# First stage of a streaming-encoder block: another reciprocal root, adaLN sums of two blocks on TensorE, and the last gate sums moved

## The chip, the cores and the metric

The kernel runs on one core of a Trainium2 chip. The metric is the device time of one execution in microseconds, as the median of several runs. The profile is that of one execution, whose own time stands beside its span.

## The reference, cut to what matters

The block takes x (1024 rows of 1024) and a conditioning row c (1024). Its first part is an adaLN-modulated RMS normalisation:

```
ada = c @ w_ada + b_ada                     # 1024 x 3072
shift, scale, gate = split(ada, 3)
h = x * rsqrt(mean(x*x, -1) + 1e-6) * norm_w * (1 + scale) + shift
proj = h @ w_in                             # cq, ckv, k_rope, gates, q_b, k_b, v_b, ...
... two attentions, gated, merged, projected back ...
x = x + gate * (merged @ w_out)
```

All arithmetic is fp32. A product of two fp32 matrices is made of three passes over a high and a low part of each operand (hi x hi, hi x lo, lo x hi). The change is about `rsqrt`, about `c @ w_ada` for the first two blocks of 128 channels (of shift and scale), and about where in the program a part of `c @ w_ada` for `gate` is summed.

## The kernel before, in words

x lies in eight tiles of 128 rows. In the first stage (`phase0`) ScalarE squares a tile and sums along its rows (`square`, L269); for each pair of tiles VectorE makes the reciprocal root and scales both tiles (`scale`, L272, L276). `rsqrt` (L84 to L97) starts from a bit trick and takes three Newton steps, eleven VectorE operations that each need the one before. TensorE then transposes a tile in eight pieces of 128x128 (`turn`, L285) into PSUM, and ScalarE copies them to xT (`evac`, L301).

A block kt is 128 channels of xT. For it the kernel needs one shift and one gain per channel, which are sums over the 1024 entries of c. There are two ways for one such sum: `ada_rows` (L303) gives it to TensorE as eight matmuls of 64 equal columns, each run in two passes (x16 in the trace), and `ada_cols` (L311) to VectorE, as a product with c (a copy of it on all partitions, cb) that sums along its row. Before, only the shift of block 0 goes by TensorE. `gain` (L315) finishes the two numbers. `high`, `modulate` and `low` (L322 to L336) make the high part of h on ScalarE, h itself, and the low part on VectorE. `products` (L344) are the three passes of the first projection (cq, 424 columns) for a block and some tiles. TensorE makes the products of blocks kt0 and kt1 for six of the eight tiles and then for the two last ones, and goes on with block kt2.

The order is written out by hand: the calls in `phase0`, one after the other, give each engine its order. All loads are issued by one queue (SP) in that order; the order of loads is thus the order of the calls `load_x`, `load` and `load_cq`. TensorE begins with 32 transposes of the identity (`warm`).

Later, with the latents made, a loop over sp (L1384) makes keys; in each of its four turns two of the eight blocks of `gate` are summed on VectorE (`gate_sum`, L873, L878). In between, `fill_to` lets TensorE do other projections (passes over b), whose results VectorE makes ready with bv_u (L830). The last sums are ahead of one of these bv_u in VectorE's order. Then `attention` opens: rope and transposes of queries and keys (q_u, k_u, ks_u, kt), and after it a fixed table of steps; `gate_row` (L882) stands in it at step (2, 0) and transposes the eight sums on TensorE.

Of the kernel before, what the change touches and what calls it, by code (L numbers as in the profile page):

```python
# [10 lines left out]
F32 = mybir.dt.float32  # L11
# [3 lines left out]
AF = mybir.ActivationFunctionType  # L15
ALU = mybir.AluOpType
# [9 lines left out]
EPS = 1e-6  # L26
# [48 lines left out]
class Net:  # L75
# [78 lines left out]
    def consts(self):  # L154
        nc, t, U = self.nc, self.t, self.U
        cp = self.cp
        self.x0 = U.get([P, D], F32, "x0")
        nc.sync.dma_start(self.x0, t["x"][0:P, :])
        self.ident = cp.tile([P, P], F32, name="ident")
        nc.sync.dma_start(self.ident, t["ident"])  # L160
        self.vec = cp.tile([P, t["vec"].shape[1]], F32, name="vec")
        nc.sync.dma_start(self.vec, t["vec"])
        self.misc_raw = self.Hs.get([P, 512], F32, "misc")
        self.pos = cp.tile([P, ST], I32, name="pos")
        self.ones = cp.tile([P, 1], F32, name="ones")
# [12 lines left out]
        self.bf_row = v[:, 41:49]
        self.b_gate = v[:, 49:57]
# [59 lines left out]
    def phase0(self):  # L239
# [11 lines left out]
        def load_x(*sts):  # L251
            for st in sts:
                xs[st] = U.get([P, D], F32, f"x{st}")
                nc.sync.dma_start(xs[st], t["x"][st * P:(st + 1) * P, :])

        def load(kt):
            wada[kt] = [U.get([P, D], F32, f"wada{kt}{e}") for e in range(2)]
            for e in range(2):
                nc.sync.dma_start(wada[kt][e], t["w_ada"][kt][:, e])

        def load_cq(gi, half=None):
            if not half:
                cqw.append(U.get([P, 2, 424], F32, f"raw_cq{gi}"))
            k = slice(0, 2) if half is None else slice(half, half + 1)
            nc.sync.dma_start(cqw[gi][:, k], t["w_cq"][:, 2 * gi + k.start:2 * gi + k.stop])

        def square(st):
            junk = Hs.get([P, 512], F32, f"junk{st}")
            nc.scalar.activation(junk.bitcast(BF16), xs[st], AF.Square, accum_out=ssq[:, st:st + 1])  # L269
            Hs.put(junk)  # L270

        def scale(pair):  # L272
            a, b = pair
            r = self.rsqrt(ssq[:, a:b + 1], 2, D, f"x{a}")
# [27 lines left out]

        def ada_rows(kt, bank):  # L303

            pa = self.bank(bank, f"pada{kt}")[:, 0:64]
            w = wada[kt][0].rearrange("p (r c) -> p r c", r=8)
            for rc in range(8):
                self.mm(pa, w[:, rc], col(rc).broadcast_to([P, 64]), rc == 0, rc == 7)
            return pa[:, 0:1]

        def ada_cols(kt, e):  # L311
            w, a = wada[kt][e], acc[:, kt, e:e + 1]
            nc.vector.scalar_tensor_tensor(out=w, in0=w, scalar=1.0, in1=self.cb, op0=ALU.mult, op1=ALU.mult, accum_out=a)

        def gain(kt, a0=None):  # L315
            a0, a1 = acc[:, kt, 0:1] if a0 is None else a0, acc[:, kt, 1:2]
            nc.vector.tensor_scalar(out=gs[:, kt, 0:1], in0=a0, scalar1=self.b_shift[:, kt:kt + 1], scalar2=None, op0=ALU.add)
            nc.vector.scalar_tensor_tensor(out=gs[:, kt, 1:2], in0=a1, scalar=self.b1[:, kt:kt + 1],
                                           in1=self.nw[:, kt:kt + 1], op0=ALU.add, op1=ALU.mult)
            U.put(*wada.pop(kt))  # L320
# [29 lines left out]
        self.gcol = self.sp.tile([P, 8], F32, name="gcol")  # L350
        load_x(1, 2, 3, 4, 5)
        load(0)
        self.cb = U.get([P, D], F32, "cb")
        nc.sync.dma_start(self.cb, t["c_row"].broadcast_to([P, D]))
        load_cq(0, 0)
        load_x(6, 7)
        load(1)
        load_cq(0, 1)
        most, last = range(6), (6, 7)
        self.warm_bank = self.bank("f", "warm")  # L360
        for st in range(5):
# [12 lines left out]
        a0 = ada_rows(0, "o")
        evac(2)
        square(6)
        ada_cols(0, 1)
        gain(0, a0)
        load(2)
        evac(3)  # L380
        wh, wl = U.get([P, 2, 424], F32R, "hi_cq0"), U.get([P, 2, 424], F32R, "lo_cq0")
        nc.scalar.copy(wh[:, 0], cqw[0][:, 0])
        high(0, range(4))
        scale((4, 5))
        modulate(0, range(4), "d")
# [3 lines left out]
        turn(4, "tt")
        evac(4)  # L390
        square(7)
        turn(5, "of")
        evac(5)
        high(0, (4, 5))
        scale((6, 7))
        accs = [self.bank("s", f"cq_s{i}") for i in range(2)]
        for st in range(4):
            banks[st] = accs[st // 2][:, st % 2 * 512:st % 2 * 512 + 512]
        products(0, range(4), (0, ))
        load(3)  # L400
        load_cq(2)
        nc.sync.dma_start(self.misc_raw[:, 0:t["misc"].shape[1]], t["misc"])
        nc.sync.dma_start(self.pos, t["pos"])
        products(0, range(4), (2, 1))
        turn(6, "tt")
        evac(6)
        turn(7, "tt")
        modulate(0, (4, 5), "d")
        low(0, (4, 5))
        banks[4], banks[5] = self.bank("o", "cq_o"), self.bank("f", "cq_f")  # L410
        products(0, (4, 5))
        ada_cols(1, 0)
        ada_cols(1, 1)
        gain(1)
        high(1, most)
        modulate(1, most, "a")
        nc.scalar.copy(wh[:, 1], cqw[0][:, 1])
        evac(7)
        nc.vector.tensor_tensor(out=wl[:, 1], in0=cqw[0][:, 1], in1=wh[:, 1].bitcast(F32), op=ALU.subtract)
        U.put(cqw[0])  # L420
        load(4)
        low(1, most)
        products(1, most)
        wh, wl = U.get([P, 2, 424], F32R, "hi_cq1"), U.get([P, 2, 424], F32R, "lo_cq1")
        ada_cols(2, 0)
        ada_cols(2, 1)
# [800 lines left out]
    def attention(self):  # L1227
# [92 lines left out]
    def build(self):  # L1320
# [91 lines left out]
def layout(i):  # L1412
# [68 lines left out]
```

## Time and profile before

| | us |
|---|---|
| median of 3 runs (lowest, highest) | 979.08 (977.92, 980.4) |
| the profiled execution's own time | 978.43 |
| its span | 976.3 |
| TensorE busy in the span | 950.1 (97%) |
| VectorE busy | 642.2 (66%) |
| ScalarE busy | 477.0 (49%) |
| GpSimd busy | 203.4 (21%) |

The span is from the first to the last instruction of the profiled execution. The idle time of an engine that waits for nothing late costs nothing; what counts is where TensorE, which is busy nearly all the time, stands still or has a lower clock. PEclk is the granted clock as a share of full speed: 1.00 is 2.4 GHz, 0.50 is 1.2 GHz. DMA shares are of 16 engines.

### The profile page before, as it was taken

How to read it: one execution, taken by the hardware profiler on the slowest of the kernel's cores; microseconds unless marked ns; L12 is line 12 of the kernel's file. 1: busy time of each engine (PE TensorE's matmuls, PEld its weight loads, DVE VectorE, ACT ScalarE, POOL GpSimd, SP SyncE). 2: the span in 40 equal slices, each digit the busy share in tenths (PEclk: the TensorE clock that was granted, in tenths of full speed). 3: DMA queues.
4: the chain of work that ended last, by engine and by line, in shares of the span. 5: the costliest groups of instructions: out<-in, count | busy, mean ns of one | idle time of the engine just before them, and what ended most of it. 6: DMA issues, size and time to landing. Idle time of an engine off the chain costs nothing.

```text
span 976.3 us, 15256 instructions
## 1 busy us (share of the span) xinstructions
PE 950.1 (97%) x5534; PEld 829.2 (85%) x5534; DVE 642.2 (66%) x1408; ACT 477.0 (49%) x955; POOL 203.4 (21%) x259
## 2 busy tenths in 40 slices
PE   5899999999999999999999999999999999999998
PEld 5799999999897887888888888888888878887887
DVE  5877877777645756667667677667676757496222
ACT  6775824443244555656555566565565644143000
POOL 0013024300002221222233323332333210045000
PEclk9999999999999999999999999999999999999999
DMA  9831032854954224225323232232411554643321
GB/s 349 312 98 44 23 109 83 295 193 160 312 163 130 87 65 109 87 65 141 98 76 100 66 88 67 93 105 88 131 56 44 184 183 151 225 152 130 105 90 65
DMA packets 80987, 124.98 MB, mean 128 GB/s; under 512 B 5928, under 2 KB 47536, under 8 KB 80912
## 3 DMA queue, kind: packets, MB, share of 16 engines
q1 hardware_dynamic: 80912, 124.01, 38.6%
q8 instruction: 43, 0.70, 0.3%
q14 instruction: 32, 0.26, 0.1%
HBM read 88.33 MB, written 35.66 MB: 127 GB/s over the span
## 4 chain that ended last, share of the span: by engine, by line
PE 62%; DVE 3%; DMA 2%; issue 1%; ACT 0%; SPq 0%; ACTq 0%; DVEq 0%
PE f L127 31%; PE out L127 9%; PE s L127 8%; PE o L127 7%; PE pt L136 6%; DMA raw_f_u<-in_w_br 1%; DVE hT_lo L986 1%; DVE mg_h L979 1%; PE kt L136 1%; PE qt L136 1%; DMA mg_h<-mg_d 1%; DVE lo_f_u L116 1%; ACT p_u L1160 0%; ACT q_u L1096 0%; ACT hi_f_u L115 0%
## 5 line engine op out<-in xcount | busy, mean ns | idle before, releaser
L1180 ACT CAST pp_u<-pt 128x512 fp32r<-128x512 f32 x192 | 91.9, 479 | 179.3 <-PE pt L136 164.1
L1181 DVE TENSOR_TENSOR pp_u<-pt,pp_u 128x512 fp32r<-128x512 f32 x192 | 106.5, 555 | 76.4 <-ACT pp_u L1180 74.5
L127 PE MATMUL f<-hT_lo,hi_f_u 128*128 128x512 f32 x384 | 153.5, 400 | 0.0
L127 PE MATMUL f<-hT_hi,lo_f_u 128*128 128x512 f32 x384 | 153.3, 399 | 0.0
L127 PE MATMUL f<-hT_hi,hi_f_u 128*128 128x512 f32 x384 | 153.3, 399 | 0.0
L127 PE MATMUL s<-k_u,q_u 96*128 96x512 f32 (+6 forms) x480 | 116.5, 362 | 2.0 <-ACT p_u L1160 1.2
L127 PE MATMUL b<-hi_b_u,hT_hi 128*128 128x256 f32 x384 | 110.4, 288 | 2.3 <-DVE bv_u L830 2.3
L127 PE MATMUL b<-lo_b_u,hT_hi 128*128 128x256 f32 x384 | 109.2, 284 | 0.0
L127 PE MATMUL b<-hi_b_u,hT_lo 128*128 128x256 f32 x384 | 109.2, 284 | 0.0
L1154 DVE TENSOR_REDUCE nm<-s 128x1 f32<-128x128 f32 (+7 forms) x128 | 97.0, 758 | 4.4
L1164 POOL TENSOR_SCALAR p_u<-p_u,rs 128x640 f32<-128x640 f32 (+1 forms) x64 | 64.4, 1006 | 166.7 <-DVE rs L1163 83.5
L127 PE MATMUL o<-pp_u,v_u 128*128 128x512 f32 (+7 forms) x384 | 94.2, 340 | 0.0
L1164 POOL TENSOR_SCALAR p_h<-p_h,rs 128x128 f32<-128x128 f32 (+1 forms) x64 | 36.7, 573 | 252.1 <-DVE rs L1163 205.9
L127 PEld LDWEIGHTS s<-k_u,q_u 96*128 96x128 f32 (+2 forms) x480 | 76.6, 190 | 7.6 <-ACT p_u L1160 1.5
L127 PEld LDWEIGHTS f<-hT_hi,lo_f_u 128*128 128x128 f32 x384 | 72.4, 189 | 11.9
L127 PEld LDWEIGHTS f<-hT_lo,hi_f_u 128*128 128x128 f32 x384 | 72.4, 189 | 11.5
L127 PEld LDWEIGHTS f<-hT_hi,hi_f_u 128*128 128x128 f32 x384 | 72.5, 189 | 11.0
L127 PEld LDWEIGHTS o<-pp_u,v_u 128*128 128x128 f32 (+1 forms) x384 | 61.7, 161 | 19.9 <-DVE pp_u L1181 0.4
L127 PEld LDWEIGHTS b<-hi_b_u,hT_hi 128*128 128x128 f32 x384 | 74.3, 193 | 2.8 <-DVE bv_u L830 2.5
L127 PEld LDWEIGHTS b<-lo_b_u,hT_hi 128*128 128x128 f32 x384 | 74.3, 194 | 0.3
L127 PEld LDWEIGHTS b<-hi_b_u,hT_lo 128*128 128x128 f32 x384 | 74.2, 193 | 0.0
L136 PEld LDWEIGHTS pt<-ident,p_u 128*128 128x128 f32 x416 | 52.7, 140 | 16.4
(306 smaller groups left out, 1997.6 us busy)
## 6 DMA issues: line engine op xcount, KB each, us to landing
raw_f_u<-in_w_t SPq DMA_DIRECT2D x24, 512.0 KB
wada_u<-in_w_ada SPq DMA_DIRECT2D x16, 512.0 KB
mg_d<-th_h SPq DMA_DIRECT2D x32, 256.0 KB
mg_h<-mg_d SPq DMA_DIRECT2D x32, 256.0 KB
raw_b_u<-in_w_b SPq DMA_DIRECT2D x12, 512.0 KB
x_u<-in_x SPq DMA_DIRECT2D x8, 512.0 KB
raw_wg_u<-in_w_gate SPq DMA_DIRECT2D x8, 512.0 KB
va_d<-vhl_u SPq DMA_DIRECT2D x8, 512.0 KB
```

The lines of the kernel that those rows point to most:

```text
L116: engine.tensor_tensor(out=lo[:, ks], in0=raw[:, ks], in1=hi[:, ks].bitcast(F32), op=ALU.subtract)
L127: self.nc.tensor.matmul(out, lhsT=l, rhs=r, start=start, stop=stop)
L136: self.nc.tensor.transpose(out=out, in_=in_, identity=self.ident)
L979: nc.vector.scalar_tensor_tensor(out=m, in0=m, scalar=1.0, in1=acc, op0=ALU.add, op1=ALU.mult)
L986: nc.vector.tensor_tensor(out=self.hT_lo[x], in0=mA[c1][:, x[2]], in1=self.hT_hi[x].bitcast(F32), op=ALU.subtract)
L1154: nc.vector.tensor_reduce(out=nm, in_=sv, axis=AX.X, op=ALU.max, negate=True)
L1164: nc.gpsimd.tensor_scalar(out=p[:, 0:w], in0=p[:, 0:w], scalar1=rs, scalar2=0.0, op0=ALU.mult, op1=ALU.add)
L1180: nc.scalar.copy(ph[:, c0:], pt[:, c0:])
L1181: nc.vector.tensor_tensor(out=pl[:, c0:], in0=pt[:, c0:], in1=ph[:, c0:].bitcast(F32), op=ALU.subtract)
```

## The change

The root of a pair of tiles is made by ScalarE's Sqrt and VectorE's reciprocal, then one Newton step; a first Sqrt of a constant is issued before the first square, so that the activation table is there. Both sums of block 0 and both of block 1 go by TensorE (four times eight narrow matmuls, where one stood). The first two pairs are scaled straight after their squares. Loads: x6 and x7 go ahead of c's row and the first projection weights, block 1's weights are loaded ahead of c's row, and block 4's ahead of two small ones. The sums of four gate blocks (4 to 7) move from the loop to the opening of `attention`, and `gate_row` from step (2, 0) to (3, 0).

```diff
@@ scale
-            r = self.rsqrt(ssq[:, a:b + 1], 2, D, f"x{a}")
+            v, y, q = (...)
+            nc.vector.tensor_scalar(out=v, in0=ssq[:, a:b + 1], scalar1=1.0 / D, scalar2=EPS, op0=ALU.mult, op1=ALU.add)
+            nc.scalar.activation(y, ssq[:, a:b + 1], AF.Sqrt, scale=1.0 / D, bias=self.eps)
+            nc.vector.reciprocal(y, y)
+            nc.vector.scalar_tensor_tensor(out=q, in0=y, scalar=-0.5, in1=y, op0=ALU.mult, op1=ALU.mult)
+            nc.vector.tensor_tensor(out=q, in0=q, in1=v, op=ALU.mult)
+            nc.vector.scalar_tensor_tensor(out=y, in0=q, scalar=1.5, in1=y, op0=ALU.add, op1=ALU.mult)
+            r = y
@@ ada_rows
-            pa = self.bank(bank, f"pada{kt}")[:, 0:64]
-            w = wada[kt][0].rearrange("p (r c) -> p r c", r=8)
-            for rc in range(8):
-                self.mm(pa, w[:, rc], col(rc).broadcast_to([P, 64]), rc == 0, rc == 7)
-            return pa[:, 0:1]
+            b = self.bank(bank, f"pada{kt}")
+            for e in range(2):
+                w = wada[kt][e].rearrange("p (r c) -> p r c", r=8)
+                for rc in range(8):
+                    self.mm(b[:, 64 * e:64 * e + 64], w[:, rc], col(rc).broadcast_to([P, 64]), rc == 0, rc == 7)
+            return b[:, 0:1], b[:, 64:65]
@@ the order of phase0
         load(0)
+        load_x(6, 7)
+        load_cq(0, 0)
+        load(1)
+        load_cq(0, 1)
         self.cb = U.get([P, D], F32, "cb")
         nc.sync.dma_start(self.cb, t["c_row"].broadcast_to([P, D]))
-        load_cq(0, 0)
-        load_x(6, 7)
-        load(1)
-        load_cq(0, 1)
+        load_cq(1)
...
-        for st in range(5):
+        nc.scalar.activation(root, self.eps, AF.Sqrt)
+        for st in range(4):
             square(st)
+            if st % 2:
+                scale((st - 1, st))
         warm(32, self.ident)
-        scale((0, 1))
...
-        a0 = ada_rows(0, "o")
         evac(2)
+        rows = ada_rows(0, "o")
+        evac(3)
+        gain(0, rows)
         square(6)
-        ada_cols(0, 1)
-        gain(0, a0)
...
-        products(0, range(4), (0, ))
+        products(0, range(4), (0, 2))
+        rows = ada_rows(1, "t")
+        modulate(0, (4, 5), "d")
+        low(0, (4, 5))
+        gain(1, rows)
+        nc.scalar.copy(wh[:, 1], cqw[0][:, 1])
+        products(0, range(4), (1, ))
...
-        ada_cols(1, 0)
-        ada_cols(1, 1)
-        gain(1)
-        high(1, most)
-        modulate(1, most, "a")
@@ attention's opening
         self.load_v(0)
+        self.gate_sum(range(4, 8))
+        self.U.put(self.cb)
@@ the loop over sp, and the table of steps
-                    self.gate_sum((2 * sp, 2 * sp + 1))
+                    if sp < 2:
+                        self.gate_sum((2 * sp, 2 * sp + 1))
...
-        self.extra += [((2, 0), self.gate_row, ())]
+        self.extra += [((3, 0), self.gate_row, ())]
```

VectorE, first pair of x in the first stage, before (v, y and a are the root's tiles, x_u a tile of x):

```order
L88 TENSOR_SCALAR v_x_182<-xssq 128x2
L89 TENSOR_SCALAR y_x_183<-v_x_182 128x2
L93 SCALAR_TENSOR_TENSOR a_x_184<-y_x_183 128x2
L95 TENSOR_TENSOR a_x_184<-a_x_184,v_x_182 128x2
L96 SCALAR_TENSOR_TENSOR y_x_183<-a_x_184,y_x_183 128x2
L93 SCALAR_TENSOR_TENSOR a_x_184<-y_x_183 128x2
L95 TENSOR_TENSOR a_x_184<-a_x_184,v_x_182 128x2
L96 SCALAR_TENSOR_TENSOR y_x_183<-a_x_184,y_x_183 128x2
L93 SCALAR_TENSOR_TENSOR a_x_184<-y_x_183 128x2
L95 TENSOR_TENSOR a_x_184<-a_x_184,v_x_182 128x2
L96 SCALAR_TENSOR_TENSOR y_x_183<-a_x_184,y_x_183 128x2
L276 TENSOR_SCALAR x_u_1_87<-x_u_1_87,y_x_183 128x1024
```

VectorE at the same place now:

```order
L278 TENSOR_SCALAR v_x_150<-xssq 128x2
L280 RECIPROCAL y_x_151<-y_x_151 128x2
L281 SCALAR_TENSOR_TENSOR a_x_152<-y_x_151 128x2
L282 TENSOR_TENSOR a_x_152<-a_x_152,v_x_150 128x2
L283 SCALAR_TENSOR_TENSOR y_x_151<-a_x_152,y_x_151 128x2
L286 TENSOR_SCALAR x_u_1_87<-x_u_1_87,y_x_151 128x1024
L286 TENSOR_SCALAR x_u_2_114<-x_u_2_114,y_x_151 128x1024
L278 TENSOR_SCALAR v_x_165<-xssq 128x2
```

Five operations lie ahead of the first scaling where eleven did, and the Sqrt that feeds the reciprocal is on ScalarE. TensorE, from the first narrow matmuls (pada) to the second group of products, before (xt are transposes, cq_s products of the first four tiles):

```order
L127 MATMUL pada_260<-vec,wada_u_7_122 128x64 x8
L136 MATMUL xt_0_305<-ident,x_u_5_118 128x128 x4
L136 MATMUL xt_1_306<-ident,x_u_5_118 128x128 x4
L136 MATMUL xt_0_319<-ident,x_u_6_120 128x128 x4
L136 MATMUL xt_1_320<-ident,x_u_6_120 128x128 x4
L127 MATMUL cq_s_348<-hi_cq_u_18_282,hT_hi 128x424 x2
L127 MATMUL cq_s_349<-hi_cq_u_18_282,hT_hi 128x424 x2
L127 MATMUL cq_s_348<-hi_cq_u_18_282,hT_lo 128x424 x2
L127 MATMUL cq_s_349<-hi_cq_u_18_282,hT_lo 128x424 x2
```

TensorE at the same place now:

```order
L127 MATMUL pada_267<-vec,wada_u_7_124 128x64 x8
L127 MATMUL pada_267<-vec,wada_u_8_125 128x64 x8
L136 MATMUL xt_0_294<-ident,x_u_5_120 128x128 x4
L136 MATMUL xt_1_295<-ident,x_u_5_120 128x128 x4
L136 MATMUL xt_0_304<-ident,x_u_6_122 128x128 x4
L136 MATMUL xt_1_305<-ident,x_u_6_122 128x128 x4
L127 MATMUL cq_s_343<-hi_cq_u_16_291,hT_hi 128x424 x2
L127 MATMUL cq_s_344<-hi_cq_u_16_291,hT_hi 128x424 x2
L127 MATMUL cq_s_343<-hi_cq_u_16_291,hT_lo 128x424 x2
L127 MATMUL cq_s_344<-hi_cq_u_16_291,hT_lo 128x424 x2
L127 MATMUL pada_353<-vec,wada_u_12_134 128x64 x8
L127 MATMUL pada_353<-vec,wada_u_13_135 128x64 x8
```

Both sums of block 0 stand ahead of the transposes of x4 and x5, and both of block 1 stand between the products of block 0. VectorE around the last two gate sums (raw_wg_u), before (bv_u makes a projection of b ready, kraw_h are keys, q_u queries):

```order
L788 TENSOR_TENSOR kraw_h_64_2984<-kraw_h_64_2984,y_g2k_3050 128x512
L788 TENSOR_TENSOR kraw_h_65_3042<-kraw_h_65_3042,y_g2k_3050 128x512
L878 SCALAR_TENSOR_TENSOR raw_wg_u_132_2878,gcol<-raw_wg_u_132_2878,cb_u_112_2410 128x1024
L878 SCALAR_TENSOR_TENSOR raw_wg_u_133_2880,gcol<-raw_wg_u_133_2880,cb_u_112_2410 128x1024
L830 TENSOR_TENSOR bv_1_u_141_3101<-b_1_3010,bv_1_u_141_3101 128x8x64
L116 TENSOR_TENSOR lo_b_1_u_143_3106<-raw_b_1_u_135_2925,hi_b_1_u_142_3105 128x512 x2
L830 TENSOR_TENSOR bv_2_u_145_3170<-b_2_3111,bv_2_u_145_3170 128x8x64
L830 TENSOR_TENSOR bv_3_u_146_3223<-b_3_3174,bv_3_u_146_3223 128x8x64
L1047 SCALAR_TENSOR_TENSOR q_0_u_150_3263<-qt_3270,vqa,q_0_u_149_3262 64x512
```

VectorE at the same place and at the new place now:

```order
L800 TENSOR_TENSOR kraw_h_64_2988<-kraw_h_64_2988,y_g2k_3054 128x512
L800 TENSOR_TENSOR kraw_h_65_3046<-kraw_h_65_3046,y_g2k_3054 128x512
L842 TENSOR_TENSOR bv_1_u_141_3103<-b_1_3014,bv_1_u_141_3103 128x8x64
L116 TENSOR_TENSOR lo_b_1_u_143_3108<-raw_b_1_u_135_2929,hi_b_1_u_142_3107 128x512 x2
L842 TENSOR_TENSOR bv_2_u_145_3172<-b_2_3113,bv_2_u_145_3172 128x8x64
L842 TENSOR_TENSOR bv_3_u_146_3225<-b_3_3176,bv_3_u_146_3225 128x8x64
L890 SCALAR_TENSOR_TENSOR raw_wg_u_126_2715,gcol<-raw_wg_u_126_2715,cb_u_112_2416 128x1024
L890 SCALAR_TENSOR_TENSOR raw_wg_u_127_2717,gcol<-raw_wg_u_127_2717,cb_u_112_2416 128x1024
L890 SCALAR_TENSOR_TENSOR raw_wg_u_132_2882,gcol<-raw_wg_u_132_2882,cb_u_112_2416 128x1024
L890 SCALAR_TENSOR_TENSOR raw_wg_u_133_2884,gcol<-raw_wg_u_133_2884,cb_u_112_2416 128x1024
L1059 SCALAR_TENSOR_TENSOR q_0_u_150_3269<-qt_3276,vqa,q_0_u_149_3268 64x512
L1059 SCALAR_TENSOR_TENSOR q_1_u_152_3273<-qt_3276,vqa,q_1_u_151_3272 64x512
```

No gate sum is ahead of the first bv_u now; four stand behind the third one, ahead of the first q_u.

## Rows read from the trace of the kernel before

**Rows 1.** The page's busy time, share of the span and instructions of each engine

```profile
PE 950.1 (97%) x5534; PEld 829.2 (85%) x5534; DVE 642.2 (66%) x1408; ACT 477.0 (49%) x955; POOL 203.4 (21%) x259
```

**Rows 2.** Windows: stretch, length, busy time, PEclk, DMA share, GB/s

```profile
10.20:20.40 10.20, 6.50 (x56) 5.89 (x54) 7.58 (x30) 8.30 (x17) 0.00 (x0) 1.00 1.03 403
20.50:27.20 6.70, 4.59 (x20) 4.55 (x21) 4.86 (x17) 4.61 (x10) 0.00 (x0) 0.50 1.04 409
259.40:262.70 3.30, 3.02 (x14) 3.02 (x15) 2.03 (x4) 0.00 (x0) 0.00 (x0) 0.50 0.98 336
270.00:278.00 8.00, 7.99 (x68) 7.80 (x67) 3.69 (x5) 3.32 (x5) 0.00 (x0) 1.00 0.92 257
```

**Rows 3.** Timeline, TensorE, 10 to 42: start, length, what, [idle before]

```profile
12.05 1.97 PE L136 MATMUL xt<-ident,x_u 128*128 128x128 f32 x16 [1.02 <-DVE x_u L276]
15.55 1.97 PE L136 MATMUL xt<-ident,x_u 128*128 128x128 f32 x16 [1.53 <-DVE x_u L276]
17.35 1.90 PE L127 MATMUL pada<-vec,wada_u 128*128 128x64 f32 x16
22.61 3.65 PE L136 MATMUL xt<-ident,x_u 128*128 128x128 f32 x16 [3.36 <-DVE x_u L276]
...
27.37 0.93 PE L127 MATMUL cq_s<-hi_cq_u,hT_lo 128*128 128x424 f32 x4
28.14 0.93 PE L127 MATMUL cq_s<-lo_cq_u,hT_hi 128*128 128x424 f32 x4
...
35.77 1.04 PE L127 MATMUL cq_s<-hi_cq_u,hT_hi 128*128 128x424 f32 x4 [2.85 <-ACT hi_cq_u L417]
...
41.83 0.93 PE L127 MATMUL cq_s<-hi_cq_u,hT_hi 128*128 128x424 f32 x4
```

**Rows 4.** Timeline, VectorE, first stage

```profile
9.07 0.17 DVE L88 TENSOR_SCALAR v_x<-xssq 128x2 f32<-128x2 f32 x1 [3.92 <-ACT junk_h L269]
...
11.24 1.42 DVE L276 TENSOR_SCALAR x_u<-x_u,y_x 128x1024 f32<-128x1024 f32 x2
...
14.74 1.42 DVE L276 TENSOR_SCALAR x_u<-x_u,y_x 128x1024 f32<-128x1024 f32 x2
...
32.95 0.21 DVE L318 SCALAR_TENSOR_TENSOR gs<-ada,b,vec 128x1 f32<-128x1 f32 x1
```

**Rows 5.** Timeline, ScalarE, first stage

```profile
8.86 0.19 ACT L269 ACTIVATION_READ_ACCUMULATOR junk_h<-x_u 128x1 f32 x1
9.13 1.06 ACT L269 ACTIVATE junk_h<-x_u 128x1024 bf16<-128x1024 f32 x1
...
18.64 1.06 ACT L269 ACTIVATE junk_h<-x_u 128x1024 bf16<-128x1024 f32 x1 [0.89 <-DMA x_u<-in_x]
```

**Rows 6.** The reciprocal's line, L1163

```profile
L1163 DVE RECIPROCAL rs<-sm x128: 145/162/165, 287.7 to 798.6; 128x1 f32<-128x1 f32 x128
```

**Rows 7.** Timeline, VectorE, 256 to 273

```profile
256.66 1.22 DVE L878 SCALAR_TENSOR_TENSOR raw_wg_u<-raw_wg_u,cb_u 128x1024 f32<-128x1024 f32 x1
...
258.94 0.68 DVE L830 TENSOR_TENSOR bv_u<-b,bv_u 128x512 fp32r<-128x512 f32 x1
...
267.70 0.69 DVE L830 TENSOR_TENSOR bv_u<-b,bv_u 128x512 fp32r<-128x512 f32 x1 [6.27 <-ACT bv_u L829]
272.55 1.53 DVE L1047 SCALAR_TENSOR_TENSOR q_u<-qt,vqa,q_u 64x512 fp32r<-64x512 f32 x2 [4.16 <-ACT q_u L1045]
```

**Rows 8.** Timeline, TensorE, the gate sums' wait and ks_u

```profile
259.68 0.58 PE L127 MATMUL b<-hi_b_u,hT_hi 128*128 128x256 f32 x1 [2.30 <-DVE bv_u L830]
...
278.01 0.63 PE L136 MATMUL kt<-ident,ks_u 128*128 128x128 f32 x4
```

**Rows 9.** Timeline, the gate row's place before, and one period later

```profile
370.51 0.27 PE L136 MATMUL pgT<-ident,gcol 128*8 128x128 f32 x1 [2.01 <-DVE gcol L885]
...
402.23 0.60 PE L136 MATMUL pt<-ident,p_h 128*128 128x128 f32 x4
...
404.93 0.16 DVE L1163 RECIPROCAL rs<-sm 128x1 f32<-128x1 f32 x1 [0.64 <-ACT p_u L1160]
```

More of the change, by code (lines that the diff above doesn't have):

```diff
@@ L166, in consts @@
         nc.gpsimd.memset(self.ones, 1.0)
+        self.eps = cp.tile([P, 1], F32, name="eps")
+        nc.gpsimd.memset(self.eps, EPS)
         v = self.vec
@@ L273, in scale @@
             a, b = pair
-            r = self.rsqrt(ssq[:, a:b + 1], 2, D, f"x{a}")
+            v, y, q = (self.sp.tile([P, 32], F32, tag=f"rs_{n}", name=f"{n}_x{a}", bufs=2)[:, 0:2] for n in "vya")
+            nc.vector.tensor_scalar(out=v, in0=ssq[:, a:b + 1], scalar1=1.0 / D, scalar2=EPS, op0=ALU.mult, op1=ALU.add)
[5 more added lines that the diff above has]
+            r = y
             for i, st in enumerate(pair):
@@ L313, in ada_cols, with gain @@
             nc.vector.scalar_tensor_tensor(out=w, in0=w, scalar=1.0, in1=self.cb, op0=ALU.mult, op1=ALU.mult, accum_out=a)
-        def gain(kt, a0=None):
-            a0, a1 = acc[:, kt, 0:1] if a0 is None else a0, acc[:, kt, 1:2]
+        def gain(kt, rows=None):
+            a0, a1 = rows or (acc[:, kt, 0:1], acc[:, kt, 1:2])
             nc.vector.tensor_scalar(out=gs[:, kt, 0:1], in0=a0, scalar1=self.b_shift[:, kt:kt + 1], scalar2=None, op0=ALU.add)
@@ L352, in phase0 @@
         load(0)
+        load_x(6, 7)
+        load_cq(0, 0)
+        load(1)
+        load_cq(0, 1)
         self.cb = U.get([P, D], F32, "cb")
         nc.sync.dma_start(self.cb, t["c_row"].broadcast_to([P, D]))
-        load_cq(0, 0)
-        load_x(6, 7)
-        load(1)
-        load_cq(0, 1)
+        load_cq(1)
         most, last = range(6), (6, 7)
         self.warm_bank = self.bank("f", "warm")
-        for st in range(5):
+        root = self.sp.tile([P, 1], F32, name="root")
+        nc.scalar.activation(root, self.eps, AF.Sqrt)
+        for st in range(4):
             square(st)
+            if st % 2:
+                scale((st - 1, st))
         warm(32, self.ident)
-        scale((0, 1))
         turn(0, "s")
@@ L367, in phase0 @@
         evac(0)
+        square(4)
+        evac(1)
         square(5)
-        scale((2, 3))
-        evac(1)
+        scale((4, 5))
         turn(2, "s")
         turn(3, "tt")
-        load_cq(1)
-        a0 = ada_rows(0, "o")
         evac(2)
+        rows = ada_rows(0, "o")
+        evac(3)
+        gain(0, rows)
         square(6)
-        ada_cols(0, 1)
-        gain(0, a0)
-        load(2)
-        evac(3)
+        high(0, range(4))
         wh, wl = U.get([P, 2, 424], F32R, "hi_cq0"), U.get([P, 2, 424], F32R, "lo_cq0")
         nc.scalar.copy(wh[:, 0], cqw[0][:, 0])
-        high(0, range(4))
-        scale((4, 5))
+        turn(4, "tt")
+        turn(5, "of")
+        load(2)
+        load(3)
         modulate(0, range(4), "d")
         low(0, range(4))
+        evac(4)
+        square(7)
+        scale((6, 7))
         nc.vector.tensor_tensor(out=wl[:, 0], in0=cqw[0][:, 0], in1=wh[:, 0].bitcast(F32), op=ALU.subtract)
         self.cqw.append((wh, wl))
[L389 to L392, printed above, removed]
         evac(5)
         high(0, (4, 5))
-        scale((6, 7))
         accs = [self.bank("s", f"cq_s{i}") for i in range(2)]
@@ L398, in phase0 @@
             banks[st] = accs[st // 2][:, st % 2 * 512:st % 2 * 512 + 512]
-        products(0, range(4), (0, ))
-        load(3)
+        products(0, range(4), (0, 2))
[5 more added lines that the diff above has]
+        products(0, range(4), (1, ))
         load_cq(2)
+        load(4)
         nc.sync.dma_start(self.misc_raw[:, 0:t["misc"].shape[1]], t["misc"])
         nc.sync.dma_start(self.pos, t["pos"])
-        products(0, range(4), (2, 1))
         turn(6, "tt")
+        high(1, most)
+        modulate(1, most, "d")
         evac(6)
-        turn(7, "tt")
-        modulate(0, (4, 5), "d")
-        low(0, (4, 5))
+        low(1, most)
         banks[4], banks[5] = self.bank("o", "cq_o"), self.bank("f", "cq_f")
         products(0, (4, 5))
-        ada_cols(1, 0)
-        ada_cols(1, 1)
-        gain(1)
-        high(1, most)
-        modulate(1, most, "a")
-        nc.scalar.copy(wh[:, 1], cqw[0][:, 1])
+        turn(7, "tt")
         evac(7)
@@ L420, in phase0 @@
         U.put(cqw[0])
-        load(4)
-        low(1, most)
-        products(1, most)
+        products(1, most, (0, 2, 1))
         wh, wl = U.get([P, 2, 424], F32R, "hi_cq1"), U.get([P, 2, 424], F32R, "lo_cq1")
@@ L437, in phase0 @@
             products(kt, last)
+        high(2)
+        modulate(2, engine="a")
         nc.vector.tensor_tensor(out=wl, in0=cqw[1], in1=wh.bitcast(F32), op=ALU.subtract)
@@ L440, in phase0 @@
         self.cqw.append((wh, wl))
-        high(2)
-        modulate(2, engine="a")
         ada_cols(3, 0)
@@ L1390, in build @@
                     self.fill_to(self.pe_time + 6500)
-                self.U.put(self.cb)
                 self.store()
@@ L1420, in layout @@
     cols = wa[:, :, 0:2].transpose(3, 4, 2, 0, 1).reshape(8, P, 2, 1024)
-    o["w_ada"] = np.concatenate([np.stack([rows[0:1, :, 0], cols[0:1, :, 1]], 2), cols[1:8]])
+    o["w_ada"] = np.concatenate([rows[0:2], cols[2:8]])
     o["w_gate"] = np.ascontiguousarray(a["w_ada"][0][:, 2048:].T.reshape(8, P, 1024))
```

## Prediction

> **What bounds the kernel now.** I read the busy shares first: TensorE works 950.1 of 976.3 us [rows 1]. From then on the question is only where TensorE doesn't run, or runs slowly, and whether the change touches it. The view of windows gives its clock: 1.00 (2.4 GHz) in 10.2 to 20.4 and 0.50 (1.2 GHz) in 20.5 to 27.2 and in 259.4 to 262.7 [rows 2]. The timeline of TensorE then gives the first stage [rows 3]. Up to 41.83, where the third block (kt2) begins, the idle times that VectorE or ScalarE end are 1.02, 1.53, 3.36 and 2.85. Sixteen transposes take 1.97 at 12.05 and 15.55, but 3.65 at 22.61, in the slow window. VectorE's timeline shows what the first idle times wait for: eleven dependent tiny operations from 9.07 to 11.24, 2.17 us or 0.197 each, stand ahead of the first scaling [rows 4]. The last, 2.85, is the chain of block 1: VectorE's sums feed the gain at 32.95, and ScalarE's three steps then end in time for 35.77. Later the only idle time of size near a changed line is 2.30 at 259.68: TensorE waits for bv_u of VectorE, which stands behind two gate sums (256.66 to 258.94, 2 x 1.14) [rows 7, 8]. After that wait the clock is at its lower level for 14 passes.
>
> **The first stage, part by part.** *Root.* v, which needs only the sums, runs beside the Sqrt of ScalarE. In the nearest row a ScalarE operation on one column takes 0.19 [rows 5]; two columns with a scale and a bias I take at 0.20, with 0.07 (the eleven-step pitch less the operation's length, twice) to hand over, and as bounds 0.15 and 0.60 (about half of the 1.06 of a 128x1024 square). The reciprocal is 0.16 [rows 6], the three Newton operations 3 x 0.197. From 9.07 the first scaling starts at 9.07 + 0.27 + 0.20 + 0.59 = 10.13 instead of 11.24: 1.1 earlier. Of that x0's transposes can use all but the warm-up's end at 12.05 - 1.02 = 11.03.
>
> *Pair of x2, x3.* Its two squares, from 9.13 on 1.06 and 0.19 each [rows 5], stand 0.2 later behind the Sqrt; they end near 11.8 and the scaling starts near 12.7 instead of 14.74: 2.0 earlier. The two tiles' transposes then end by 15.83 (16 at 0.11 from 13.5, and half a microsecond in which the second tile waits for ScalarE to copy a PSUM bank out), where before they end at 17.35: 1.5 earlier.
>
> *From there to kt2.* I worked each engine's new order forward with the durations of before. TensorE finds its inputs ready all the way, though twice with almost no margin: the first product's two operands come at 21.1 (narrow multiplies end 15.83 + 3.6 = 19.4, gain 0.3, then ScalarE's two steps), and TensorE gets to it at 21.16; the low part comes at 21.94 against 21.93. x6, whose transfer ends ScalarE's wait of 0.89 at 18.64 [rows 5], is now queued ahead of the row of c and half of the first projection weights, 512 + 212 KB; at the 403 GB/s of that stretch [rows 2] this brings it 1.8 earlier. Block 1's weights are read only near 24. VectorE gives up three block sums and six root operations for each of four pairs, and takes over block 1's modulation from ScalarE; neither engine is the later one there by this working. So TensorE's time is its own work: 64 narrow passes where 16 stood (1.90 for 16, or 0.112 each [rows 3]) 7.2, 32 transposes at 0.11 3.5, and 48 products at 0.19 (four between 27.37 and 28.14 [rows 3]) 9.2. That is 19.9, from 15.83 to 35.7, against 41.83: 6.1 earlier. The same adding up of before from 17.35 (two waits of 6.2, 1.7 for the slow transposes, 14.6 of work) falls 2.0 short of its 24.5: slow products and short waits and hand-overs that have no row here. A quarter of that, 0.5, I charge to the new order, and so take 5.6, with 4.9 and 6.4 as ends. The 48 extra narrow passes cost 5.4 and are in it; what pays for them is the idle time that goes (3.36 + 2.85, and 1.5 ahead of it) and the slow stretch. After 41.83 TensorE was without a long wait up to 257, so the gain is carried on; blocks kt2 and kt3 keep their sums on VectorE, which has no transpose of TensorE waiting for it by then.
>
> *A rule on transposes.* In the traced kernel TensorE has done nothing but transposes ahead of 12.05, and yet 16 of them take 1.97 there, with a granted clock of 1.00 [rows 2, 3]. The Trainium skill, "TensorE: Matmul & The Clock Gate", section "Part 4: PE-mode transpose", says the contrary: such transposes don't count as busy and don't bring the full clock. By that rule the opening, which now holds only transposes and narrow multiplies, would stay slow, and this kernel would come out slower (the third rival).
>
> **The gate sums.** Taken out of VectorE's order ahead of bv_u, they let it start at 256.66 instead of 258.94; it takes 0.68 and is done at 257.34, and TensorE needs it at 259.68 - 2.30 = 257.38. So the wait of 2.30 goes. Without a wait I expect no fall of the clock behind it: 14 passes take 3.02 at 0.50 [rows 2], at full clock half: 1.35 to 1.5 gone, taken 1.35. At their new place four sums of 1.14 are 4.6 us; VectorE stands idle 6.27 ahead of 267.70 and 4.16 ahead of 272.55 [rows 7]. They are queued behind the 267.70 row, so they end near 273.0 and hold the q_u of 272.55 behind them up 0.4; the scores that read it come behind the kt transposes of 278.01, 5 us of cover (without it: 0.4). The last four gate weights and the copy of c keep their buffers up to 30 us longer; the loads that come next take others that are free by then, in the order of the program, so I count nothing (a late load of block weights, if I am wrong: up to 1). What is late next is ks_u: its transposes at 278.01 [rows 8] start just when its transfer lands, in a stretch with a DMA share of 0.92 [rows 2]; being 3.65 earlier there TensorE may wait 0 to 1 us. I take 0.45. Sum: 2.30 + 1.35 - 0.45 = 3.2, with ends 1.9 and 3.8.
>
> **The gate row.** It moves from where TensorE waits 2.01 for gcol [rows 9] to one period later. There the transposes in front of it end at 402.23 + 0.60, and VectorE's addition stands behind a reciprocal of 404.93, which gives about 2.3. I count 0.3 of loss, with ends 2.0 gain (nothing to wait for) and 0.6 loss.
>
> **Sum.** The profiled execution took 978.43 (span 976.3 and 2.1 around it). 978.43 - 5.6 - 3.2 + 0.3 = 969.9; the median of the runs, 979.08, stands 0.65 above it, so 970.6.
>
> **The rivals.** *1. The clock falls behind the narrow multiplies.* For: it fell at 20.42, after the one group of narrow multiplies of before (17.35 to 19.25), and a narrow pass moves half of a transpose's columns in the same time; now there are two groups of twice the length. Against: in both slow windows of before TensorE had stood idle for more than 1 us ahead of the fall, and in the forecast it doesn't. Price: behind the first group stand 16 transposes (3.65 - 1.97 = 1.7), behind the second four products and eight transposes (4 x 0.19 + 8 x 0.105 = 1.6). One fall gives 972.3, both 973.9. *2. The second gain is taken by transfers:* ks_u and the rope pieces land no earlier, in a stretch that is full of transfers. For: the DMA share of 0.92 to 278 [rows 2]. Against: the loads' own issue moves forward with the work that they wait for. Price: up to the 3.2 less what the clock gives, so 972 to 973.8. *3. The clock stays low from the opening to the first products' end near 26.4* (slower than before). Place: TensorE from 11 to 26. Price by rows: 48 transposes at 0.105 more (1.68/16) 5.0, 64 narrow passes at 0.1 more (were they to double) 6.5, eight products at 0.19 more 1.5, together 13.0: 983.6. It decides the sign once the loss passes 979.1 - 970.6 = 8.5 us. Against: the 1.97 at 12.05 and at 15.55. The section "Part 4: PE-mode transpose" of the Trainium skill's page "TensorE: Matmul & The Clock Gate" would lead here; no run shown so far does.
>
> **How the numbers follow.** A difference under 0.3%, 2.9 us, can't be told from none here: faster is below 976.1, slower above 982.0. Forecast 0.60 (its own ends 967.8 to 972); rival 1 0.22; rival 2 0.11; rival 3 0.03; 0.04 for pieces of several that leave 974 to 981. The range 967.5 to 975.5 takes in the first three. Faster 0.93, same 0.04, slower 0.03.
>
> **What would show it.** In the profile after: the first 128x1024 scaling near 10.1; narrow multiplies from 15.8; a granted clock of 1.00 from 11 to 36; kt2's products at 35.5 to 36.5; no TensorE wait at bv_u and none at the second window's place, the gate sums inside VectorE's idle time; a wait of up to 1 ahead of kt<-ks_u; the gate row's transpose behind a wait near 2.3. A 0.50 window between 18 and 30 makes rival 1 right, a wait of 2 or more at ks_u rival 2. The prediction is wrong if kt2 starts after 38 or the stretch from kt2 to the first kt<-ks_u isn't 2 to 4 us shorter.

## The result and the profile after

| | before | changed |
|---|---|---|
| median (lowest, highest), us | 979.08 (977.08, 980.6), 5 runs | 973.2 (970.77, 974.52), 5 runs |
| profiled execution's own time, us | 978.43 | 970.98 |
| its span, us | 976.3 | 969.0 |

The changed kernel is faster: the ratio is 0.9936, with a 95% interval from 0.9911 to 0.996. The median lies inside the range (967.5 to 975.5), 2.6 us above the predicted 970.6. The profiled execution is one of the shorter ones of the changed kernel.

TensorE's timeline of the changed kernel, first stage (start, length, what, idle time before it and what ended it), answers [rows 3]:

```profile
10.66 1.91 PE L136 MATMUL xt<-ident,x_u 128*128 128x128 f32 x16
12.82 1.09 PE L136 MATMUL xt<-ident,x_u 128*128 128x128 f32 x8 [0.25 <-DVE x_u L286]
14.38 1.14 PE L136 MATMUL xt<-ident,x_u 128*128 128x128 f32 x8 [0.48 <-ACT xT L311]
15.37 3.68 PE L127 MATMUL pada<-vec,wada_u 128*128 128x64 f32 x32
18.89 1.92 PE L136 MATMUL xt<-ident,x_u 128*128 128x128 f32 x16
20.83 1.03 PE L127 MATMUL cq_s<-hi_cq_u,hT_hi 128*128 128x424 f32 x4
21.70 1.05 PE L127 MATMUL cq_s<-hi_cq_u,hT_lo 128*128 128x424 f32 x4
22.59 3.68 PE L127 MATMUL pada<-vec,wada_u 128*128 128x64 f32 x32
...
35.57 0.93 PE L127 MATMUL cq_s<-hi_cq_u,hT_hi 128*128 128x424 f32 x4
```

The waits of 3.36 and 2.85 are gone, and no row behind that of 14.38 has an idle time. The row at 35.57 is kt2; before it stood at 41.83. The windows of the same kernel answer [rows 2] (columns as there):

```profile
10.20:20.40 10.20, 9.48 (x84) 8.93 (x83) 5.53 (x19) 9.24 (x20) 0.00 (x0) 1.00 1.02 392
20.50:27.20 6.70, 6.67 (x50) 6.14 (x49) 4.86 (x14) 4.74 (x11) 0.00 (x0) 1.00 1.02 397
250.00:258.00 8.00, 8.00 (x69) 8.00 (x69) 1.54 (x4) 1.17 (x2) 0.00 (x0) 1.00 1.02 307
395.60:398.80 3.20, 3.20 (x11) 2.50 (x11) 0.68 (x1) 1.62 (x3) 0.00 (x0) 0.50 0.90 220
```

The granted clock is 1.00 through both groups of narrow multiplies and behind bv_u, where before it was 0.50. A new stretch at 0.50 stands at 395.6. VectorE's timeline shows the root and the gate sums, as [rows 4, 7] do of before:

```profile
8.36 0.17 DVE L278 TENSOR_SCALAR v_x<-xssq 128x2 f32<-128x2 f32 x1 [3.29 <-ACT junk_h L271]
8.69 0.17 DVE L280 RECIPROCAL y_x<-y_x 128x2 f32<-128x2 f32 x1 [0.16 <-ACT y_x L279]
...
9.48 1.42 DVE L286 TENSOR_SCALAR x_u<-x_u,y_x 128x1024 f32<-128x1024 f32 x2
...
12.01 1.41 DVE L286 TENSOR_SCALAR x_u<-x_u,y_x 128x1024 f32<-128x1024 f32 x2
...
248.22 0.68 DVE L842 TENSOR_TENSOR bv_u<-b,bv_u 128x512 fp32r<-128x512 f32 x1
...
257.25 0.69 DVE L842 TENSOR_TENSOR bv_u<-b,bv_u 128x512 fp32r<-128x512 f32 x1 [5.07 <-ACT bv_u L841]
257.86 1.22 DVE L890 SCALAR_TENSOR_TENSOR raw_wg_u<-raw_wg_u,cb_u 128x1024 f32<-128x1024 f32 x1
...
262.44 1.51 DVE L1059 SCALAR_TENSOR_TENSOR q_u<-qt,vqa,q_u 64x512 fp32r<-64x512 f32 x2
```

From the sums (8.36) to the first scaling (9.48) it is now 1.12 us instead of 2.17, with 0.16 of idle time for the Sqrt. bv_u runs without gate sums ahead of it, and the gate sums end as q_u begins. Two places further on answer [rows 8, 9], in TensorE's timeline:

```profile
269.11 0.63 PE L136 MATMUL kt<-ident,ks_u 128*128 128x128 f32 x4 [1.58 <-DMA ks_u<-ka_d]
...
394.11 0.27 PE L136 MATMUL pgT<-ident,gcol 128*8 128x128 f32 x1 [2.40 <-DVE gcol L897]
```

TensorE's matmuls are the same in both kernels from kt2 on, but for the place of pgT and the order of some near it. So their starts, matmul by matmul, show where the lead comes and goes: 6.3 us at kt2 and 6.6 a few us later; 9.0 at bv_u (259.68 against 250.67) and 10.4 behind the old slow stretch; 8.9 at kt (278.01 against 269.11), where the new wait of 1.58 is paid; 8.4 behind the gate row, whose two waits are 2.01 and 2.40; 6.9 behind the 0.50 stretch that follows it, which thus costs 1.6; 7.5 behind a wait near 786 for p_u, which ScalarE makes in the attention (1.24 before, 0.49 here); 7.35 at the end (7.3 in the spans).

### The profile page after: what moved, and what is told of

Its sections match the earlier page's. It is cut to its first block, busy times and chain, and to the rows that moved or that the text cites. A ratio compares the mean times of both kernels' runs of the same rounds, so it can differ in the third digit from the quotient of the medians.

```text
span 969.0 us, 15332 instructions
## 1 busy us (share of the span) xinstructions
PE 952.2 (98%) x5582; PEld 832.3 (86%) x5582; DVE 636.0 (66%) x1379; ACT 477.6 (49%) x959; POOL 204.0 (21%) x260
## 4 chain that ended last, share of the span: by engine, by line
PE 89%; DVE 4%; DMA 3%; ACT 2%; issue 2%; POOL 0%; SPq 0%; ACTq 0%; DVEq 0%
PE f L127 31%; PE b L127 12%; PE out L127 9%; PE s L127 9%; PE o L127 7%; PE pt L136 6%; PE q L127 3%; PE ckv L127 2%; PE kv L127 2%; PE cq_s L127 2%; DVE hT_lo L998 1%; DMA ks_u<-ka_d 1%; PE cq_t L127 1%; DVE mg_h L991 1%; PE pada L127 1%
```

## The experiments

Each kernel was timed in several runs beside runs of the kernel before, whose medians were 979.08 (first four kernels), 979.26 (next four) and 979.81 (last two). All edits are to the changed kernel unless it says otherwise.

**again: the changed kernel, unedited.**

> The changed kernel once more, unedited, to see where its runs differ: they lay at 970.8 to 971.0 with a mean clock of 0.998 and at 973.2 to 974.5 with 0.996. Theory: the work is the same and one more stretch at half clock, some 4 us long, costs the 2 to 3.5 us; all runs again 970 to 975. Rival: the spread is of transfers, and the clock has nothing to do with it. If the trace is of the longer kind: by the prediction's first rival its extra 0.50 stretch lies between 15 and 30 us, behind the narrow multiplies; by another it lies later, behind a wait.

Measured: 974.14 (970.12 to 977.35, 6 runs), 0.9946 (0.9926 to 0.9966). The trace is of a longer run (974.81). Its timeline of TensorE, and its windows:

```profile
270.03 1.09 PE L136 MATMUL kt<-ident,ks_u 128*128 128x128 f32 x4 [2.21 <-DMA ks_u<-ka_d]
```

```profile
270.10:273.30 3.20, 3.20 (x16) 3.20 (x17) 0.72 (x1) 1.37 (x2) 0.00 (x0) 0.50 0.22 79
```

The first stage ran as in the first trace, at 1.00 (kt2 0.3 later). The wait for ks_u was 2.21 instead of 1.58, and here the clock fell behind it: the matmuls that follow lose another 1.45 against the first trace up to 273.3. Together 2.1 of the 3.9 us between the two traces; another 0.8 comes from waits near 786. So the difference between these two traces lies mainly at ks_u, not in the first stage. The mean clock doesn't sort the runs as the text above says: of the first five, that of 974.08 has 0.998 too. So a second slow stretch isn't shown for each of the longer runs.

**first_only and sums_only: the two halves of the change.** first_only puts the gate sums and the gate row back:

```diff
@@ attention's opening
-        self.gate_sum(range(4, 8))
-        self.U.put(self.cb)
...
@@ the table of steps
-        self.extra += [((3, 0), self.gate_row, ())]
+        self.extra += [((2, 0), self.gate_row, ())]
...
@@ the loop over sp
-                    if sp < 2:
-                        self.gate_sum((2 * sp, 2 * sp + 1))
+                    self.gate_sum((2 * sp, 2 * sp + 1))
...
```

> The changed kernel, with the gate sums and the gate row where they were before. Theory: kt2 starts at 35.6 as in the changed kernel, 6.3 earlier than before, and the wait of 2.30 for bv_u stands again with a 0.50 stretch behind it: 6.0 to 6.5 less than before, 972.6 to 973. Rival: the first stage's gain is partly lost on the way to 257 us (a late load): under 5 less.

Measured: 972.79 (972.16 to 974.32), 0.994 (0.9927 to 0.9952). kt2 starts at 35.52, and the old wait stands again, with a stretch at 0.50 behind it:

```profile
253.08 0.39 PE L127 MATMUL b<-hi_b_u,hT_hi 128*128 128x256 f32 x1 [2.30 <-DVE bv_u L842]
```

```profile
253.70:257.00 3.30, 3.30 (x18) 3.30 (x17) 1.13 (x2) 0.00 (x0) 0.00 (x0) 0.50 1.06 370
```

sums_only is the kernel before, with only the gate sums moved as in the change:

> The kernel before, with nothing of the change but the move of gate sums 4 to 7 into the opening of attention (gate row still at (2, 0)). Theory: the wait of 2.30 for bv_u and the half-clock stretch behind it (1.35) go, and a wait for ks_u of 1.0 to 1.6 comes: 2.0 to 2.7 less than before, 976.5 to 977. Rival: transfers take all of it back: under 0.5 less. Rival with the other sign: none of the move helps and gcol comes late at (2, 0): 1 more.

Measured: 977.99 (974.89 to 980.92, 11 runs), 0.9984 (0.9969 to 0.9998). TensorE's timeline and the window behind it:

```profile
275.16 0.63 PE L136 MATMUL kt<-ident,ks_u 128*128 128x128 f32 x4 [1.90 <-DMA ks_u<-ka_d]
```

```profile
276.00:279.20 3.20, 3.20 (x17) 3.20 (x16) 1.87 (x3) 2.17 (x4) 0.00 (x0) 0.50 0.06 21
```

By the medians the first stage alone gives 6.3, and the gate sums alone 1.1, below the 2.0 to 2.7 expected (the interval of their ratio, 0.2 to 3.0 us, takes these in). The trace of sums_only shows why it is so little: 3.9 us are won by 264, and the wait for ks_u and the slow stretch behind it take 3.4 of them back. A wait and a slow stretch did not go away, they went to ks_u. (Another 0.8 that this trace is ahead by comes from its first stage, where the slow stretch was 3.4 us long instead of 6.8; no edit touches that.) The whole change (973.2 and 974.14) is no better than first_only.

**add_early: gcol is ready before it is asked for.**

```diff
         self.gate_sum(range(4, 8))
         self.U.put(self.cb)
+        self.nc.vector.tensor_tensor(out=self.gcol, in0=self.gcol, in1=self.b_gate, op=ALU.add)
...
     def gate_row(self):
-        nc.vector.tensor_tensor(out=self.gcol, in0=self.gcol, in1=self.b_gate, op=ALU.add)
```

> The changed kernel, with the addition to gcol put right behind the four gate sums instead of directly ahead of the gate row's transpose at step (3, 0). Theory: in the trace TensorE stood 2.40 us for this addition, which was queued behind a reciprocal on VectorE, and the granted clock then fell to 0.50 for some 3 us, 1.4 lost; both go, so 3.8 less than the changed kernel (967 for the short kind of run). Rival: the wait is only handed to the next thing that needs VectorE, and the clock falls elsewhere: under 1 us less.

Measured: 968.49 (966.88 to 972.25), 0.9898 (0.9881 to 0.9915). Its timeline at the gate row, and a window around it:

```profile
390.16 0.27 PE L136 MATMUL pgT<-ident,gcol 128*8 128x128 f32 x1
```

```profile
389.00:397.00 8.00, 8.00 (x45) 6.72 (x44) 6.36 (x15) 4.52 (x8) 1.92 (x2) 1.00 0.39 86
```

No idle time ahead of pgT, and the clock stays at 1.00. In this trace the wait for ks_u was 0.51, with nothing done to any load: how late ks_u lands differs from run to run.

**late_v: the load of v behind ks_u.**

```diff
-        self.load_v(0)
         self.gate_sum(range(4, 8))
...
-        for _ in range(5):
+        for i in range(5):
             next(preps[0])
+            if i == 3:
+                self.load_v(0)
```

> The changed kernel, with the load of v (512 KB) issued behind ks_u and the k_u pieces instead of ahead of the q_u pieces. Theory: TensorE's wait for ks_u (1.58 and 2.21 in two traces, the second with a 0.50 stretch of 3.4 us behind it) is there because ks_u lands behind 512 KB that nobody needs yet; ks_u lands some 1.3 us earlier, the wait goes down to 0 to 0.5, no clock falls there, and the runs near 974 go: median 970.5 to 971.5. Rival: the pieces share the engines anyway and ks_u lands no earlier: 973 to 974 again. Rival with the other sign: v comes late for its first product: over 974.

Measured: 970.61 (967.85 to 971.4), 0.99 (0.9886 to 0.9914). The two rows of TensorE's timeline:

```profile
267.57 0.60 PE L136 MATMUL kt<-ident,ks_u 128*128 128x128 f32 x4
...
392.54 0.27 PE L136 MATMUL pgT<-ident,gcol 128*8 128x128 f32 x1 [2.39 <-DVE gcol L897]
```

The wait for ks_u is gone in this trace, as expected, and no run is above 971.4. The wait for gcol stands as before, but in this trace the clock stayed at 1.00 behind it.

**best: both edits.**

> Both edits: the addition to gcol behind the gate sums, and the load of v behind ks_u and k_u. Theory: the two losses are of different places and add: 3.8 less for the gate row's wait and fall, 1.6 to 3.0 less for ks_u: 965.5 to 968. Rival: with the gate row's wait gone in the run before, the rest of the spread came from elsewhere (786 us and the end), and the load of v changes nothing: 968.5 as before.

Measured: 966.73 (966.2 to 967.27, 4 runs), 0.9868 (0.9856 to 0.9881). Both rows are without idle time:

```profile
267.42 0.60 PE L136 MATMUL kt<-ident,ks_u 128*128 128x128 f32 x4
...
389.82 0.27 PE L136 MATMUL pgT<-ident,gcol 128*8 128x128 f32 x1
```

What is left in this trace is a wait near the end for mg_h, which VectorE makes for the last projection. It stands in every trace of this case (1.10 to 2.27 us), here with a stretch at 0.50 behind it that costs 1.6:

```profile
872.29 0.50 PE L127 MATMUL out<-hi_wo_u,hT_hi 128*128 128x512 f32 x1 [1.93 <-DVE mg_h L990]
```

```profile
873.60:876.80 3.20, 3.20 (x9) 2.52 (x8) 2.55 (x4) 1.89 (x5) 0.66 (x1) 0.50 0.00 0
```

The median with both edits beats that of the changed kernel by 6.5 us, and the four runs lie within 1.1 us, where those of the changed kernel lie within 7.2 (11 runs).

**old_root: eleven operations again.**

```diff
-            nc.scalar.activation(y, ssq[:, a:b + 1], AF.Sqrt, scale=1.0 / D, bias=self.eps)
...
+            r = self.rsqrt(ssq[:, a:b + 1], 2, D, f"x{a}")
```

> The changed kernel with the old root of eleven VectorE operations in all four pairs, the rest of the first stage's order as changed. Theory: the first scaling comes 1.05 later, the second pair's 2.0, TensorE's narrow multiplies begin 1.5 later (16.9 for 15.37) and from there nothing waits: kt2 at 37.1, 1.5 more than the changed kernel. Rival: the new waits make the clock fall in the first stage and cost 1.5 to 3 more: kt2 at 38.5 or later. Rival: the root's cover is full and nothing is lost: kt2 at 35.6.

Measured: 975.48 (974.05 to 978.29), 0.9961 (0.9946 to 0.9975). TensorE's timeline:

```profile
11.69 1.97 PE L136 MATMUL xt<-ident,x_u 128*128 128x128 f32 x16 [0.96 <-DVE x_u L279]
15.18 1.97 PE L136 MATMUL xt<-ident,x_u 128*128 128x128 f32 x16 [1.52 <-DVE x_u L279]
16.99 3.68 PE L127 MATMUL pada<-vec,wada_u 128*128 128x64 f32 x32
...
28.89 1.03 PE L127 MATMUL cq_s<-lo_cq_u,hT_hi 128*128 128x424 f32 x4 [0.99 <-DVE lo_cq_u L399]
...
38.38 0.93 PE L127 MATMUL cq_s<-hi_cq_u,hT_hi 128*128 128x424 f32 x4
```

The narrow multiplies begin at 16.99, as expected; kt2 comes at 38.38, 1.3 later than the theory said, most of it a wait of 0.99 for lo_cq, which stands behind the fourth pair's longer root on VectorE. The clock did not fall in this stage (it did behind the wait for mg_h, at 880). By kt2's start the new root is worth 2.8 of the stage's 6.3. By the medians it is worth 1.3 to 2.3 (973.2 and 974.14 for the changed kernel), and the intervals overlap.

**cols1: block 1's sums on VectorE.**

```diff
...
-        rows = ada_rows(1, "t")
...
-        gain(1, rows)
+        ada_cols(1, 0)
+        ada_cols(1, 1)
+        gain(1)
```

> The changed kernel with block 1's two sums on VectorE, as before (c's row is loaded ahead of block 1's weights), and 32 narrow passes fewer on TensorE. Theory: VectorE's sums end near 28.9, the high part of block 1 near 30.2; TensorE comes there 3.6 earlier, near 26.2, waits 3 to 4 and so gains nothing: kt2 at 35.9 to 36.5, plus 1.5 if the clock falls behind the wait. Rival: narrow passes are what the stage is bound by and VectorE has room: kt2 at 33 to 34, 2 less than the changed kernel.

Measured: 974.07 (971.91 to 978.42), 0.9938 (0.9924 to 0.9953). TensorE's timeline and the window behind the wait:

```profile
26.07 1.06 PE L127 MATMUL cq_s<-lo_cq_u,hT_hi 128*128 128x424 f32 x4 [3.18 <-DVE lo_cq_u L406]
```

```profile
27.40:30.70 3.30, 3.26 (x12) 2.60 (x10) 2.20 (x7) 1.32 (x2) 0.00 (x0) 0.50 1.03 403
```

With 32 narrow passes fewer TensorE gains nothing: it waits 3.18, earlier than I had said, for lo_cq, which VectorE makes at the same time as in the changed kernel (25.42 and 25.27). Behind that wait the clock fell, and kt2 starts at 37.64 in this trace, 2.1 later. That is the longest of its six runs (978.42); behind this stretch three more stand at 0.50, behind the waits for ks_u (2.13), gcol (2.40) and p_u (1.23). The median lies 0.9 above the changed kernel's first and 0.1 below its second, and isn't told apart from them. So the narrow multiplies of block 1 fill a hole, and in a run like the traced one they keep the clock up.

**row_20: the gate row at its old step.**

```diff
-        self.extra += [((3, 0), self.gate_row, ())]
+        self.extra += [((2, 0), self.gate_row, ())]
```

> The changed kernel with the gate row at step (2, 0), where it was before. Theory: in four traces with the row at (3, 0) TensorE waited 2.40 for gcol and the clock then fell for 3.4 us in three of them; in three traces with the row at (2, 0) it waited 2.0 and the clock stayed at 1.00. So 0.4 and most of 1.4 less than the changed kernel, 1.2 to 1.8: 971.4 to 972.5. Rival: the fall there is chance, and the place is worth only the 0.4: 973 to 974.

(The count in this text is wrong: of five traces with the row at (3, 0) the clock fell in three.) Measured: 972.93 (969.95 to 976.38), 0.9934 (0.9917 to 0.9951). TensorE's timeline and the window behind it:

```profile
360.49 0.27 PE L136 MATMUL pgT<-ident,gcol 128*8 128x128 f32 x1 [2.01 <-DVE gcol L897]
```

```profile
361.30:364.50 3.20, 3.20 (x12) 2.43 (x10) 2.51 (x4) 2.21 (x4) 0.25 (x1) 0.50 0.04 9
```

The theory falls: here the clock fell behind the 2.01 too, and the time is that of the changed kernel. No more than the 0.4 of its wait is shown for the step of the gate row.

**sums_fixed: the gate part alone, with both mends.** The kernel before with the moved sums, the early addition and the late load of v.

> The kernel before, with the move of the gate sums, the addition to gcol right behind them, and the load of v behind ks_u and k_u; the first stage and the gate row's step as before. Theory: the move alone won 1.1 because ks_u and a fall of the clock took its 3.65 back; without that wait, and without the 2.0 ahead of the gate row, 3.65 + 2.0 = 5.6 less than before: 973 to 974. Rival: the first stage's 6.3 is needed for the loads to be early enough, and the wait for ks_u stays: 976 or more.

Measured: 972.92 (971.43 to 977.98), 0.9944 (0.9924 to 0.9964). Its timeline of TensorE:

```profile
274.74 0.63 PE L136 MATMUL kt<-ident,ks_u 128*128 128x128 f32 x4 [0.57 <-DMA ks_u<-ka_d]
```

A wait of 0.57 is left, no fall of the clock follows, and with both mends the gate part is worth 6.9 by the medians, where as it stands in the change it was worth 1.1 alone and nothing beside the first stage. The trace (971.73) is ahead of that of the kernel before by 5.2 us behind the gate row, about what the theory adds up to less the 0.57. Another 1.2 comes from shorter waits for p_u and mg_h near the end, which the edits weren't made for.

## Why the prediction was right, and where its terms were off

**Root.** Right. 1.06 us from the sums to the first scaling were worked out, 1.12 measured; the second pair's scaling was put near 12.7 and came at 12.01 (x1 landed 0.7 earlier in this execution). The Sqrt took 0.29 where 0.20 was taken. old_root shows the step's worth at kt2, 2.8 us, more than the 1.6 by which TensorE's narrow multiplies begin later, since the fourth pair's root holds lo_cq up as well.

**Narrow multiplies back to back.** Right: 64 passes took 7.4 (7.2 said), the stretch from them to kt2 20.2 (19.9, and 0.5 charged). So 0.3 of the 0.5 for hand-overs was used up, and the narrow multiplies began 0.5 earlier than worked out (15.37 for 15.83; 15.13 to 15.70 in seven traces). The gain was 6.3 at kt2 and 6.6 a few us later, where 5.6 was taken.

**Rival 1** (clock behind the narrow multiplies) didn't happen in any of the seven traces with the new first stage in full, nor in old_root's; in cols1, with fewer of them, the clock fell, but behind a wait of 3.18. **Rival 3** is refuted with it: after the warm-up the transposes of the opening ran at 1.00 (16 in 1.91 at 10.66), as the 1.97 of [rows 3] had said. The Trainium skill's sentence that led there ("TensorE: Matmul & The Clock Gate", section "Part 4: PE-mode transpose") is not borne out by these traces. (It speaks of transposes alone; that an opening with narrow multiplies would stay slow too was a step of the prediction's own, and this one ran at 1.00.)

**Gate sums.** The wait of 2.30 and the slow stretch went: 3.9 between the first stage and 262 (3.65 said). At their new place the sums filled VectorE's idle time ahead of q_u to its end, as worked out.

**The steps that failed.** Two terms were mis-sized. "I take 0.45" for the wait at ks_u: it was 1.58 and 2.21 in the two traces of the changed kernel. Rival 2 had its place and cause right; by its own sign (a wait of 2 or more) it is wrong in the first trace and right in the second. The argument against it (the loads' issue moves forward too) held for the issue, 10.0 earlier, as the two rows of the queue show, before and now:

```profile
268.85 0.47 SPq L1027 DMA_DIRECT2D ks_u<-ka_d  x1
```

```profile
258.81 0.38 SPq L1039 DMA_DIRECT2D ks_u<-ka_d  x1
```

It did not hold for the landing, which came only 8.9 earlier: from its issue ks_u took 9.0 us before, and 10.2 and 10.8 in the two traces of the changed kernel. And "I count 0.3 of loss" for the gate row: the wait grew by 0.4, as worked out, but 1.6 more went in a stretch at 0.50 behind it. The prediction charged a fall of the clock to the wait that went away, and none to the waits that it expected itself to come or stay. With what was measured the sum is 978.43 - 6.6 - 3.9 + 1.6 + 0.4 + 1.6 = 971.5; the rest of the difference to 970.98 is mainly the wait near 786, which was 0.75 shorter.

That the profiled execution came within 1.1 us of the 969.9 worked out for it is thus in part luck: the first stage gave 1.0 more than was taken, the place of bv_u 0.25 and that wait 0.75, against 1.1 more lost at ks_u and 1.7 at the gate row. The median, 973.2, lies outside the forecast's own ends (967.8 to 972) and inside rival 2's 972 to 973.8; it is the range over three cases that held. In the traced run of 974.81 a fall behind ks_u comes on top.

**What stays open.** Whether the clock falls behind a given wait. Its length doesn't decide it: the clock fell behind a wait of 1.23 for p_u (cols1, and not behind six as long in other traces) and stayed at 1.00 behind the 2.85 of the kernel before, in the window from 27.30 to 41.80 us. Behind gcol it stayed after 2.01 (before, first_only, sums_only) and fell after 2.01 (row_20); after 2.40 it fell in three traces and stayed in two. Behind ks_u it fell after 1.90, 2.13 and 2.21, and stayed after 1.58 and less. Behind mg_h it fell after 1.86 and 1.93 (old_root, best), and stayed after 2.27 (sums_only).

Nor was it settled why ks_u lands at another time in each run. With v behind it, it took 8.0 and 8.4 us from its issue (late_v, best), less than the 9.0 to 10.8 of the changed kernel and of add_early and row_20, which have the same loads. But it took 9.5 in sums_fixed with v behind it, and 7.5 in first_only with v ahead, so the place of v isn't all of it. And no run takes apart what the first stage gains beside the root: both sums of block 0 on TensorE, and the new order of loads and scalings.

## What to carry to other kernels

A wait that is taken away is worth its length and the slow clock behind it, and a wait that comes in its place can cost both as well: ask of each wait that will be left whether the clock falls behind it. When an engine comes earlier to a transfer, look at what is queued ahead of that transfer and not needed yet (one 512-KB load put back brought some 2 to 3 us here). An operation that only finishes a sum belongs behind the sum, not directly ahead of its reader on a busy engine (one addition of 128x8, moved, brought some 4 to 5 us).

## What the runs showed of the hardware that was not expected

The stretches at 0.50 behind a wait in the middle of the kernel were each about 3.4 us long (259.4 to 262.8 before; 395.5 to 398.9 after), and each cost 1.4 to 1.6. The clock stayed at 1.00 through 3.5 us of narrow multiplies with nothing else on TensorE, twice in each trace of the new first stage.
